# One hybrid trunk layer: mixer A's softmax on paired PSUM banks, its normalising on GpSimd, PSUM pooled anew per mixer

## Chip, cores and metric

The kernel runs as one launch on one core of a Trainium2 chip. The metric is the device time of the whole launch in microseconds; lower is better. The median of three runs of the kernel before is 1003.18 us.

## What is computed

One layer of a diffusion backbone for 128 context tokens and 512 latent tokens, model width 1024, everything in float32 at the interfaces:

```
h = RMSNorm(x) * (1 + scale1) + shift1
aq, ak, av, bq, bk, bv, ga, gb = split(h @ w_in)        # A: 8 query heads on 2 key heads; B: 8 heads
A: softmax(q k / 8) v over 512 latent + 128 cached keys  # a 128 x 640 score tile per head and query tile
B: the same over a window of the latent grid (with a learned bias) + 128 cached keys   # 384 or 512 wide
m = sigmoid(ga) * (A @ w_br_a) + sigmoid(gb) * (B @ w_br_b);  x = x + gate1 * (m @ w_out)
x = x + gate2 * (relu(h2 @ w1) ** 2 @ w2),  h2 = RMSNorm(x) * (1 + scale2) + shift2;  final RMSNorm
```

Context tokens attend to context keys only.

## The kernel before, in words

All activations lie with features on the 128 partitions and the 640 tokens along the free axis, in two halves of 320 (`HT`). A float32 product is made of three fast ones: each operand is cut into a high and a low part, and `gemm_k` (L335) adds high x high (L339), high x low (L340) and low x high (L341). One "half tile" of a weight tile is 8 of these triples into one PSUM bank. A weight tile is loaded by SyncE (L235), its high part is made by ScalarE (L301) and its low part by GpSimd or VectorE (L302); for the input projection it is GpSimd, one 128x1024 subtraction (`WPOOLSET`).

The attention stage lies at about 75 to 350 us, mixer A first (to about 220), then mixer B. For every head it goes over four query tiles. `HeadA.S` (L629) makes one 128x640 score tile as two banks of 320 columns, two matmuls each (L639, L640); VectorE takes a maximum of each bank (L641) and the smaller of the two negated ones (L642); ScalarE takes two exponentials with row sums (L644); VectorE adds the sums (L645); `normalise` (L616) takes the reciprocal (L618) and multiplies the tile on VectorE (L619). `HeadA.T` (L650) then turns the four probability tiles of a head around on TensorE (L653), `p_split` cuts them into a high part on ScalarE (L606) and a low part on VectorE (L607), and the product with the values goes into `po` (L660, L661). `HeadB` has one bank per score tile, a fused bias and maximum (L696), one exponential (L699), and the same `normalise`. `CtxPair` does the context queries of two heads.

`attention` (L921) pipelines by one head: step i of a head issues `T(i)` of the head before, `S(i)` of this one, the value product of the last `T`, and then `F.spend`, which issues some matmuls of the other input-projection tiles, the filler (`fill_tile`, L788), up to a budget (`STEP`). Mixer A's stage issues eight filler tiles, that is 16 half tiles (those of `AFILL`, and the first of `BFILL`); the last head pair has none left. A half tile is read out of its bank by ScalarE (L813, or L553 and VectorE's L554 for mixer B's queries). `F.posts` holds what follows a tile: norm and rotary of queries (L532 to L560), mixer B's key stacks (L565, L566), value stacks (L594 to L599).

PSUM has one pool for the whole kernel, by tag: `g` 2 banks (filler), `s` 3 (scores), `t` 2 (transposes), `o` 1 (value products); the norm of a query tile and the transposes of a value tile take a `g` bank too. The order of the instructions on each engine in this stage is not written by hand: the framework's planner simulates the program with its own costs and lets each engine take the earliest traced instruction that is ready. GpSimd has, beside the low parts, the low parts of mixer A's queries (L560) and DMA issues of its own queue (L577, L824, L838).

Of the kernel before, what the change touches and what calls it, by code (L numbers as in the profile page):

```python
# [10 lines left out]
F32 = mybir.dt.float32  # L11
# [5 lines left out]
P = 128  # L17
NT = 640          # tokens: 128 context, then 512 latent (column-major on the grid)
HT = 320          # tokens per half
KT = 8            # feature tiles of the model width  # L20
EPS = 1e-6
FIRST = (4, 0, 5)                                 # input tiles: mixer A keys, first queries, values
AFILL = (1, 10, 2, 6, 3, 14, 21)                      # ... next to mixer A
BFILL = (11, 7, 15, 12, 8, 16, 13, 9, 17, 29, 22, 30)         # ... next to mixer B
# [33 lines left out]
def trunk_layer(ctx: ExitStack, tc: tile.TileContext, xT, small_in, wmodA, wmodB, tabs, cacheK, cacheV, bias,  # L58
# [10 lines left out]
    pp = ctx.enter_context(tc.tile_pool(name="pp", bufs=1, space=bass.MemoryType.PSUM))  # L69
# [27 lines left out]

    def ps_g():
        return pp.tile([P, 512], F32, tag="g", bufs=2, name="pg")

    def ps_s():
        return pp.tile([P, 512], F32, tag="s", bufs=3, name="pss")

    def ps_t():
        return pp.tile([P, 512], F32, tag="t", bufs=2, name="pt")

    def ps_o():
        return pp.tile([P, 512], F32, tag="o", bufs=1, name="po")
# [55 lines left out]
    def sq_add(acc, x, f, sl):  # L164
        """sum of squares over the feature tiles but the last, whose squares are returned"""
        q = acc if f == 0 else u("sq")
        ACT.activation(q[:, sl], x[:, sl], AF.Square)
        if 0 < f < KT - 1:
            DVE.tensor_add(acc[:, sl], acc[:, sl], q[:, sl])
        return q  # L170
# [32 lines left out]
    later = []                                       # work put off until the next product  # L203
# [10 lines left out]
    class Weights:  # L214
        def __init__(self):
            self.order = list(w_order())
            self.pos = {k: i for i, (k, _) in enumerate(self.order)}
            self.loads = []                              # (key, source, number of the pair's tile)
            for key, src in self.order:
                if key[0] in BLOCKS:  # L220
                    if src is not None and key[0] == "A11":
                        self.loads += [((key[1], e), src[e], e) for e in range(2)]
                else:
                    self.loads.append((key, src, 0))
            self.st, self.t, self.raw = {}, {}, {}
            self.nd = self.nc = self.live = self.nb = 0
            self.busy = [0, 0]
# [22 lines left out]
        def block(self, name, i):  # L250
            """one operand of the seven products, [hi | lo]"""
# [37 lines left out]
        def conv(self):  # L289
            self.feed()  # L290
            key = self.order[self.nc][0]
            if key[0] in BLOCKS:
                self.t[self.nc] = self.block(*key)
            else:
                st = self.free(key)
                if key in EXTRA:
                    hi, lo = (cur["p"].tile([P, KT, P], F32R, tag="w4" + x, bufs=1, name="w4") for x in "hl")
                else:
                    hi, lo = (wp.tile([P, KT, P], F32R, tag="w" + x, bufs=3, name="w" + x) for x in "hl")
                    self.live += 2  # L300
                ACT.activation(hi, st, AF.Copy)  # L301
                (nc.gpsimd if key in WPOOLSET else DVE).tensor_sub(lo, st, r32(hi))  # L302
                self.t[self.nc] = (hi, lo)
# [10 lines left out]
        def done(self, *key):  # L314
            """the use of one tile is over; prepare the next one"""
# [39 lines left out]
    def modulate(todo, rstd, h, between=None):  # L355
        """for each (dst, x, s, sh): dst = the two parts of x * s * rstd + sh"""
# [22 lines left out]
    def warm(n):  # L379
        """keeps the tensor engine's clock up while it has to wait"""  # L380
# [3 lines left out]
    def mod_product(f, q):  # L384
        """silu(c) @ w_mod for the shift and scale of feature tile f; partial sums in four column groups"""
# [34 lines left out]
    def first_gemm(f, i, part):  # L420
        """the products of h's part with one weight tile; both parts of the tile take the high part of h"""
# [105 lines left out]
    def qk_norm(raw, g, h, bank=ps_g, src=None, buf=None):  # L527
# [23 lines left out]
    def q_part(qs, e, sl, src):  # L551
        """hi of src / 8 in the head's own partitions, lo in the other ones"""
# [4 lines left out]
    def qa_part(qs, e, raw, eng):  # L557
        """the same of mixer A's queries, whose gain holds the 1 / 8"""
# [3 lines left out]
    def k_part(k, e, dst, src, eng=None):  # L562
        """own half of the stacks k[0] = [hi; hi], k[1] = [lo; lo]"""
# [4 lines left out]
    def k_both(k, e, dst, src):  # L568
        """both halves of the stacks, the other one by the engines as well"""
# [13 lines left out]
    def v_stack(raw, cvp, bank=ps_g):  # L583
        """per key tile (ctx, lat 0..3, cache): [hi 64 | lo 64] of each of the pair's heads; in two pieces"""
# [25 lines left out]
    def combine(dst, ps, n):  # L610
        """dst (64 partitions, float32) = ps[0:64] + ps[64:128]"""
# [4 lines left out]
    def normalise(p, sm):  # L616
        rc = small("rc", 1)
        DVE.reciprocal(rc, sm)  # L618
        DVE.tensor_scalar(p, p, rc, None, op0=OP.mult)  # L619

    class HeadA:
        """512 latent queries of one head of mixer A on the latent and the cached keys"""
# [6 lines left out]
        def S(self, qt):  # L629
# [4 lines left out]
            ps = [ps_s(), ps_s()]  # L634
            p = u("pa")
            n2, s2, nm, sm = small("n2"), small("s2"), small("nm", 1), small("sm", 1)
            for j in range(2):
                c = slice(P + j * HT, P + (j + 1) * HT)
                PE.matmul(ps[j][:, :HT], q, kh[:, c], start=True, stop=False)  # L639
                PE.matmul(ps[j][:, :HT], q, kl[:, c], start=False, stop=True)  # L640
                DVE.tensor_reduce(n2[:, j:j + 1], ps[j][:, :HT], axis=AX.X, op=OP.max, negate=True)  # L641
            DVE.tensor_tensor(nm, n2[:, 0:1], n2[:, 1:2], op=OP.min)  # L642
            for j in range(2):
                ACT.activation(p[:, HALVES[j]], ps[j][:, :HT], AF.Exp, bias=nm, accum_out=s2[:, j:j + 1])  # L644
            DVE.tensor_add(sm, s2[:, 0:1], s2[:, 1:2])  # L645
# [21 lines left out]
    BQ = ((P, 384, 1, 256), (P, 512, 0, 0), (384, 512, 0, 128), (512, 384, 1, 0))   # keys, width, bias tile, columns  # L667
    BL = (0, 0, 1, 2)                                        # first local key tile of each query tile
    BG = (((4, 0, 4),), ((0, 0, 2), (3, 2, 4)), ((1, 0, 3),), ((2, 1, 4),))         # (key tile, query tiles)

    class HeadB:
        """512 latent queries of one head of mixer B on their window and the cached keys"""
# [56 lines left out]
    class CtxPair:  # L729
        """the context queries of two heads on the context keys"""  # L730
# [56 lines left out]
    # the other input tiles, interleaved with attention  # L787
    def fill_tile(n, F):  # L788
# [7 lines left out]
        for h in range(2):  # L796
# [17 lines left out]
            F.flush(1)  # L814
        F.flush()
# [32 lines left out]
    class Filler:  # L848
        """projection work that runs between the steps of attention, as far as memory allows"""
# [25 lines left out]
        def spend(self, ns):  # L875
            self.debt += ns
            while self.debt > 0:
                c = self.step()
                if c is None:
# [15 lines left out]
    # mixer A's keys, first queries and values, from the tiles computed with the first norm  # L895
# [22 lines left out]
    k_both(AK[1], 1, slice(0, NT), kraw)  # L918
    F.spend(EARLY)

    def attention(units):  # L921
        prev = pend = None
        for cur_u in units + [None]:
            if cur_u is not None:
# [54 lines left out]
    def late_mods():  # L979
        """shifts, scales and gates but the first norm's, on VectorE"""  # L980
# [30 lines left out]
    def mod_pace(used, pe=3220):  # L1011
        """as many steps as VectorE has time for next to one product"""
# [65 lines left out]
    def order(n, tail):  # L1078
        """units (tile, half): the last `tail` tiles with the first half ahead"""
# [5 lines left out]
    def unit(w, x, h):  # L1085
        """one product of a weight tile with half the tokens, with pieces of side work in its midst and behind it"""
# [50 lines left out]
    def relu2(dst, src, h):  # L1137
        """the two parts of relu(src) ** 2"""
# [15 lines left out]
    # Winograd's form of a 2 x 2 product: feature tiles 0-3 and 4-7, token halves, two weight tiles  # L1154
# [49 lines left out]
    def winograd(i, hid):  # L1204
        """hidden tiles i, i + 1 by seven products of half the depth and half the tokens"""
# [69 lines left out]
def _tiles(w, n0, n1):  # L1275
    """[K, N] -> [tiles of 128 columns, 128, K] with the contraction index k * 128 + p at [p, k, n]"""
# [18 lines left out]
def _bias_index():  # L1295
    """indices into [15 * 31 relative offsets | masked | zero]: [128 queries, 1280 key columns]"""
# [75 lines left out]
```

## Time and profile before

| | |
|---|---|
| runs | 1003.18, 1002.87, 1005.73 us; median 1003.18 us |
| span of the profiled execution, first to last instruction | 1001.3 us; the page gives the span alone, so the median lies 1.9 us over it |
| TensorE (PE) busy | 955.0 us, 95% |
| VectorE (DVE) busy | 705.0 us, 70% |
| ScalarE (ACT) busy | 517.6 us, 52% |
| GpSimd (POOL) busy | 173.5 us, 17% |
| DMA | 108.47 MB, mean 108 GB/s |

Busy time is the union of an engine's instructions. Matmuls are pipelined: each has a row of some 300 ns, and one follows the other in half of that, so TensorE can be busy by its rows without running dense; the number of matmuls per microsecond of a stretch tells the rest. An instruction's row includes the time in which it holds its engine and waits for a port.

### The profile page before, as it was taken

Reading aid. Unit: us, or ns where it says so; the run is one execution under the profiler, and the core shown is the slowest. Engines: PE = TensorE matmul, PEld = TensorE weight load, DVE = VectorE, ACT = ScalarE, POOL = GpSimd, SP = SyncE. Lnnn points to the kernel's source line nnn. Section 1 sums busy time; section 2 is a strip of 40 time slices with the busy share of each in tenths; the row PEclk is TensorE's granted clock in tenths of the full one; section 3 lists DMA queues with packets and bytes.
Section 4 is the critical chain, followed back from the end, with each engine's and each line's share of the span. In section 5 each row is a group of like instructions: output and inputs, shape, how many; then the busy total and the mean of one; then the engine's idle time right before and its main releaser. Section 6 shows DMA issues by size and latency. Waiting matters only on the chain.

```text
span 1001.3 us, 16554 instructions
## 1 busy us (share of the span) xinstructions
PE 955.0 (95%) x6317; PEld 908.8 (91%) x6317; DVE 705.0 (70%) x1576; ACT 517.6 (52%) x1117; POOL 173.5 (17%) x154
## 2 busy tenths in 40 slices
PE   7979899999899999999999999999999999999996
PEld 5778778978889999999998899999999999999896
DVE  4479898788866789788587677778733884368644
ACT  5475676668655564654324564237611662156542
POOL 0352232212231011201132100012200220012100
PEclk9999899999999999999999899999999999999999
DMA  9942101312543455556742153212320233120302
GB/s 347 208 172 69 31 25 44 77 43 77 135 111 103 133 160 189 181 169 185 224 126 81 47 164 110 85 43 84 106 78 28 85 106 88 60 79 29 126 22 105
DMA packets 34767, 108.47 MB, mean 108 GB/s; under 512 B 4320, under 2 KB 8032, under 8 KB 34688
## 3 DMA queue, kind: packets, MB, share of 16 engines
q1 hardware_dynamic: 27072, 82.63, 26.5%
q0 software_dynamic: 6464, 23.47, 8.1%
q10 hardware_dynamic: 1152, 1.31, 0.4%
q8 instruction: 49, 0.80, 0.3%
q14 instruction: 30, 0.25, 0.1%
HBM read 99.14 MB, written 4.60 MB: 104 GB/s over the span
## 4 chain that ended last, share of the span: by engine, by line
PE 65%; DVE 15%; ACT 8%; issue 3%; DMA 1%; POOL 0%; ACTq 0%; DVEq 0%; POOLq 0%; SPq 0%
PE pg L339 7%; PE pg L340 7%; PE pg L341 7%; PE pss L340 7%; PE pss L341 7%; PE pss L339 6%; PE pt L339 4%; PE pt L341 4%; PE pt L340 4%; DVE sr L260 3%; ACT wb L280 2%; PE pt L653 1%; PE pt L710 1%; DMA wst<-w 1%; DVE n L641 1%
## 5 line engine op out<-in xcount | busy, mean ns | idle before, releaser
L301 ACT ACTIVATE wh<-wst 128x1024 fp32r<-128x1024 f32 x84 | 88.8, 1057 | 112.4 <-PE pg L340 37.9
L302 DVE TENSOR_TENSOR wl<-wst,wh 128x1024 fp32r<-128x1024 f32 x53 | 64.8, 1223 | 67.5 <-ACT wh L301 67.4
L302 POOL TENSOR_TENSOR wl<-wst,wh 128x1024 fp32r<-128x1024 f32 x31 | 75.1, 2423 | 160.0 <-ACT wh L301 151.5
L992 DVE SCALAR_TENSOR_TENSOR mt<-wmt,cb 128x512 f32<-128x512 f32 x128 | 81.4, 686 | 0.0
L281 POOL TENSOR_TENSOR wb<-wst,wb 128x512 fp32r<-128x512 f32 x24 | 31.7, 1322 | 263.4 <-ACT wb L280 226.6
L339 PE MATMUL pss<-hidh,wh 128*128 128x320 f32 x216 | 67.0, 310 | 0.7 <-ACT hidh L1143 0.7
L340 PE MATMUL pss<-hidl,wh 128*128 128x320 f32 x216 | 67.0, 310 | 0.3
L341 PE MATMUL pss<-hidh,wl 128*128 128x320 f32 x216 | 66.7, 309 | 0.0
L607 DVE TENSOR_TENSOR pl<-pt,ph 128x512 fp32r<-128x512 f32 (+2 forms) x80 | 50.5, 633 | 18.3 <-ACT ph L606 17.3
L606 ACT ACTIVATE ph<-pt 128x512 fp32r<-128x512 f32 (+2 forms) x80 | 44.2, 555 | 28.8 <-PE pt L710 11.7
L280 ACT ACTIVATE wb<-sr 128x512 fp32r<-128x512 f32 x48 | 29.8, 627 | 51.5 <-DVE sr L260 35.6
L1150 DVE TENSOR_TENSOR hidl<-rl,hidh 128x320 fp32r<-128x320 f32 x64 | 37.5, 586 | 25.2 <-ACT hidh L1143 24.6
L988 POOL DMA_DIRECT2D wmt<-wmodB x32 | 17.1, 536 | 174.6 <-DVE mt L992 108.0
L340 PE MATMUL pg<-hidl,wh 128*128 128x320 f32 x144 | 44.7, 310 | 2.2 <-DVE hidl L1150 2.2
L281 DVE TENSOR_TENSOR wb<-sr,wb 128x512 fp32r<-128x512 f32 x48 | 36.0, 755 | 14.2 <-ACT wb L280 14.1
L339 PE MATMUL pg<-hidh,wh 128*128 128x320 f32 x144 | 44.7, 310 | 0.0
L341 PE MATMUL pg<-hidh,wl 128*128 128x320 f32 x144 | 44.5, 309 | 0.0
L340 PE MATMUL pt<-hidl,wh 128*128 128x320 f32 x136 | 42.1, 310 | 1.1 <-DVE hidl L1150 1.1
L341 PE MATMUL pt<-hidh,wl 128*128 128x320 f32 x136 | 42.0, 309 | 0.0
L339 PE MATMUL pt<-hidh,wh 128*128 128x320 f32 x136 | 42.0, 309 | 0.0
L644 ACT ACTIVATE pa<-pss,nm 128x320 f32<-128x320 f32 x64 | 33.1, 522 | 17.2 <-DVE nm L642 17.0
L339 PEld LDWEIGHTS pss<-hidh,wh 128*128 128x128 f32 x216 | 40.5, 188 | 1.5 <-ACT hidh L1143 1.5
(957 smaller groups left out, 3469.9 us busy)
## 6 DMA issues: line engine op xcount, KB each, us to landing
wst<-w SPq DMA_DIRECT2D x64, 512.0 KB, 3.6
wmt<-wmodB POOLq DMA_DIRECT2D x32, 512.0 KB, 4.2
wst<-w_in SPq DMA_DIRECT2D x31, 512.0 KB, 3.6
ms<-wmodA SPq DMA_DIRECT2D x16, 512.0 KB, 8.8
x<-xT SPq DMA_DIRECT2D x16, 320.0 KB, 6.1
bt<-bias SPq DMA_DIRECT2D x16, 320.0 KB, 3.3
wst<-w_br SPq DMA_DIRECT2D x8, 512.0 KB, 4.4
wst<-w_out SPq DMA_DIRECT2D x8, 512.0 KB, 3.5
```

The costliest lines, as they stand in the source:

```text
L280: ACT.activation(t[:, lo4], src, AF.Copy)
L281: later.append(lambda: (nc.gpsimd if name in BLKP else DVE).tensor_sub(t[:, hi4], src, r32(t[:, lo4])))
L301: ACT.activation(hi, st, AF.Copy)
L302: (nc.gpsimd if key in WPOOLSET else DVE).tensor_sub(lo, st, r32(hi))
L339: PE.matmul(ps, wh[:, k], xh[:, sl], start=first, stop=False)
L340: PE.matmul(ps, wh[:, k], xl[:, sl], start=False, stop=False)
L341: PE.matmul(ps, wl[:, k], xh[:, sl], start=False, stop=last)
L606: ACT.activation(ph[:, :n], pt[:, :n], AF.Copy)
L607: DVE.tensor_sub(pl[:, :n], pt[:, :n], r32(ph[:, :n]))
L644: ACT.activation(p[:, HALVES[j]], ps[j][:, :HT], AF.Exp, bias=nm, accum_out=s2[:, j:j + 1])
L992: DVE.scalar_tensor_tensor(t, st[:, q * 512:(q + 1) * 512], 1.0, r32(cb[2 * q + i][:, :512]), op0=OP.mult, op1=OP.mult, accum_out=parts[:, ...
L1150: DVE.tensor_sub(dst[1][:, sl], r[:, :HT], r32(dst[0][:, sl]))
```

## The change

In mixer A's stage the eight banks are pooled anew as two pairs for scores (`S`, 2 x 2 banks), two for transposes, one for value products and one for the filler; ahead of mixer B the pool of before is opened again. A bank of a new pool waits only for the old tiles that lay on it. A score tile of mixer A is one pair, with one maximum over both banks and one exponential. `normalise` multiplies on GpSimd, for mixer A and mixer B. The filler yields 0 behind each half tile, and in mixer A's stage `spend` returns there, with its remaining budget kept for the next step. GpSimd's low part of an input-projection tile is made in two 128x512 pieces. Norms of queries and transposes of values take a `t` bank where the pairs are in use. (Comments that the change removes are left out.)

```diff
-    pp = ctx.enter_context(tc.tile_pool(name="pp", bufs=1, space=bass.MemoryType.PSUM))
+    banks = ExitStack()
+    ctx.callback(banks.close)
+    BANKS = {"pp": {"g": 2, "s": 3, "t": 2, "o": 1}, "pa": {"S": 2, "t": 2, "o": 1, "g": 1}}
+    psum = {}
+
+    def open_banks(kind, name):
+        banks.close()
+        psum["p"] = banks.enter_context(tc.tile_pool(name=name, bufs=1, space=bass.MemoryType.PSUM, reuse_waits="tile"))
+        psum["n"] = BANKS[kind]
+
+    open_banks("pp", "pp")
...
+    def ps_2():
+        return psum["p"].tile([P, 2, 512], F32, tag="S", bufs=2, name="pss")
+
     def ps_s():
-        return pp.tile([P, 512], F32, tag="s", bufs=3, name="pss")
+        return ps_("s", "pss") if "s" in psum["n"] else ps_2()[:, 0]
...
-                (nc.gpsimd if key in WPOOLSET else DVE).tensor_sub(lo, st, r32(hi))
+                if key in WPOOLSET:
+                    for ks in (slice(0, 4), slice(4, KT)) if key[0] == "in" else (slice(0, KT),):
+                        nc.gpsimd.tensor_sub(lo[:, ks], st[:, ks], r32(hi[:, ks]))
+                else:
+                    DVE.tensor_sub(lo, st, r32(hi))
...
+    def ps_x():
+        return ps_t() if "S" in psum["n"] else ps_g()
+
-    def qk_norm(raw, g, h, bank=ps_g, src=None, buf=None):
+    def qk_norm(raw, g, h, bank=ps_x, src=None, buf=None):
-    def v_stack(raw, cvp, bank=ps_g):
+    def v_stack(raw, cvp, bank=ps_x):
...
     def normalise(p, sm):
         rc = small("rc", 1)
         DVE.reciprocal(rc, sm)
-        DVE.tensor_scalar(p, p, rc, None, op0=OP.mult)
+        nc.gpsimd.tensor_scalar(p, p, rc, None, op0=OP.mult)
...
-            ps = [ps_s(), ps_s()]
+            ps = ps_2()[:, :, :HT]
             p = u("pa")
-            n2, s2, nm, sm = small("n2"), small("s2"), small("nm", 1), small("sm", 1)
+            nm, sm = small("nm", 1), small("sm", 1)
             for j in range(2):
                 c = slice(P + j * HT, P + (j + 1) * HT)
-                PE.matmul(ps[j][:, :HT], q, kh[:, c], start=True, stop=False)
-                PE.matmul(ps[j][:, :HT], q, kl[:, c], start=False, stop=True)
-                DVE.tensor_reduce(n2[:, j:j + 1], ps[j][:, :HT], axis=AX.X, op=OP.max, negate=True)
-            DVE.tensor_tensor(nm, n2[:, 0:1], n2[:, 1:2], op=OP.min)
-            for j in range(2):
-                ACT.activation(p[:, HALVES[j]], ps[j][:, :HT], AF.Exp, bias=nm, accum_out=s2[:, j:j + 1])
-            DVE.tensor_add(sm, s2[:, 0:1], s2[:, 1:2])
+                PE.matmul(ps[:, j], q, kh[:, c], start=True, stop=False)
+                PE.matmul(ps[:, j], q, kl[:, c], start=False, stop=True)
+            DVE.tensor_reduce(nm, ps, axis=AX.XY, op=OP.max, negate=True)
+            ACT.activation(p.rearrange("p (a b) -> p a b", a=2), ps, AF.Exp, bias=nm, accum_out=sm)
             normalise(p, sm)
...
             F.flush(1)
+            yield 0
         F.flush()
...
                 c = self.step()
+                if c == 0 and "S" in psum["n"]:
+                    return
                 if c is None:
...
+    open_banks("pa", "pa")
     F.spend(EARLY)
...
         for cur_u in units + [None]:
+            if isinstance(cur_u, HeadB) and "S" in psum["n"]:
+                pend()
+                pend = None
+                open_banks("pp", "pb")
```

More of the change, by code (lines that the diff above doesn't have):

```diff
@@ L96, in small, with ps_ @@
         return sp.tile([P, n], F32, tag=f"s{n}", bufs=bufs, name=name)
+    def ps_(tag, name):
+        return psum["p"].tile([P, 512], F32, tag=tag, bufs=psum["n"][tag], name=name)
     def ps_g():
-        return pp.tile([P, 512], F32, tag="g", bufs=2, name="pg")
+        return ps_("g", "pg")
+    def ps_2():
+        return psum["p"].tile([P, 2, 512], F32, tag="S", bufs=2, name="pss")
     def ps_s():
-        return pp.tile([P, 512], F32, tag="s", bufs=3, name="pss")
+        return ps_("s", "pss") if "s" in psum["n"] else ps_2()[:, 0]
     def ps_t():
-        return pp.tile([P, 512], F32, tag="t", bufs=2, name="pt")
+        return ps_("t", "pt")
     def ps_o():
-        return pp.tile([P, 512], F32, tag="o", bufs=1, name="po")
+        return ps_("o", "po")
     def r32(ap):
```

## Prediction, made before the changed kernel was run

> **What bounds the kernel now.** I read the page first, then the busy times by stretch, then the chain, the waits and the groups of mixer A's stretch.
>
> ```profile
> span 1001.3 us, 16554 instructions
> ...
> PE 955.0 (95%) x6317; PEld 908.8 (91%) x6317; DVE 705.0 (70%) x1576; ACT 517.6 (52%) x1117; POOL 173.5 (17%) x154
> ...
> PE 65%; DVE 15%; ACT 8%; issue 3%; DMA 1%; POOL 0%; ACTq 0%; DVEq 0%; POOLq 0%; SPq 0%
> ```
>
> By busy time TensorE is full, yet a quarter of the chain that ended last is VectorE and ScalarE. The busy times by stretch say where (x is the number of instructions):
>
> ```profile
> core 0: us, PE busy (x) PEld busy (x) DVE busy (x) ACT busy (x) POOL busy (x), PEclk, DMA share, GB/s
> 75.00:220.00 145.00, 133.61 (x788) 116.39 (x788) 120.39 (x310) 93.79 (x255) 36.64 (x26) 0.95 0.19 49
> 220.00:300.00 80.00, 74.12 (x473) 66.70 (x473) 62.42 (x179) 52.50 (x133) 20.63 (x18) 1.00 0.39 101
> 300.00:350.00 50.00, 50.00 (x333) 46.77 (x332) 33.78 (x94) 28.99 (x70) 4.56 (x5) 1.00 0.38 119
> 600.00:700.00 100.00, 100.00 (x683) 100.00 (x683) 75.65 (x147) 45.50 (x88) 9.53 (x7) 1.00 0.26 84
> ```
>
> Per matmul mixer A's stretch takes 145 / 788 = 184 ns, mixer B's first part 80 / 473 = 169 and its last part, a similar mix with TensorE never idle, 50 / 333 = 150. At 150 ns mixer A's 788 would need 118 us: 27 us could be won there, and 473 x 19 ns = 9 in mixer B. The MLP's stretch (146 ns) gives nothing, and the change leaves it alone. VectorE is busy 83% of mixer A's stretch, the nearest to a bound beside TensorE. The chain by line there, and in its second half:
>
> ```profile
> by line: PE pg L339 7.7%; PE pg L340 7.2%; PE pt L653 7.2%; PE pg L341 7.1%; DVE n L641 6.7%; PE pss L639 5.2%; ACT pa L644 5.1%; DVE pl L607 4.8%; DVE pa L619 4.5%; PE po L661 4.5%; DVE nm L642 4.4%; PE po L660 4.1%; PE pss L640 3.2%; DVE
> ...
> by line: PE pg L339 7.2%; PE pg L341 7.1%; PE pg L340 6.8%; PE pt L653 6.6%; ACT pa L644 6.6%; DVE n L641 6.5%; DVE pa L619 6.3%; PE pss L639 5.4%; PE po L661 5.2%; DVE pl L607 4.7%; DVE sm L645 4.3%; DVE nm L642 4.1%; DVE bkl L566 3.5%; is
> ```
>
> So the softmax's VectorE steps are on the chain, and one of them is a minimum of two numbers per partition. The groups and one timeline show why it costs so much:
>
> ```profile
> L641 DVE TENSOR_REDUCE n<-pss 128x1 f32<-128x320 f32 x64 | 30.8, 483 | 7.1 <-PE pss L640 6.9
> L619 DVE TENSOR_SCALAR pa<-pa,rc 128x640 f32<-128x640 f32 x32 | 17.6, 551 | 0.2
> L642 DVE TENSOR_TENSOR nm<-n 128x1 f32<-128x1 f32 x32 | 10.1, 315 | 0.1
> L645 DVE TENSOR_TENSOR sm<-s 128x1 f32<-128x1 f32 x32 | 8.6, 269 | 5.3 <-ACT pa L644 5.0
> L566 DVE TENSOR_TENSOR bkl<-raw,bkh 64x512 fp32r<-64x512 f32 x4 | 3.1, 776 | 0.1
> ...
> 205.36 2.56 POOL L302 TENSOR_TENSOR wl<-wst,wh 128x1024 fp32r<-128x1024 f32 x1 [9.84 <-ACT wh L301]
> 205.62 2.33 DVE L642 TENSOR_TENSOR nm<-n 128x1 f32<-128x1 f32 x1
> ```
>
> The minimum begins 0.26 us behind GpSimd's subtraction and ends with it (207.95 against 207.92): a VectorE operation on two SBUF operands stands still while GpSimd works in SBUF.
>
> **The change part by part, mixer A.** The minimum goes: 4.4% of 145 us = 6.4 us of chain. The sum's addition goes: 4.3% of the half's 70 us = 3.0 (more, if the first half has some). Two maxima become one over 640 columns, and two exponentials one. For their slopes:
>
> ```profile
> L696 DVE CUSTOM_DVE_ANT_0 pss<-pss,bt 128x512 f32<-128x512 f32 x16 | 11.0, 687 | 0.6 <-issue 0.3 <-PE pss L693 0.3
> L696 DVE CUSTOM_DVE_ANT_0 pss<-pss,bt 128x384 f32<-128x384 f32 x15 | 8.3, 556 | 5.8 <-PE pss L693 5.7
> L699 ACT ACTIVATE pb<-pss,nm 128x512 f32<-128x512 f32 x16 | 11.0, 686 | 3.9 <-DVE nm L698 3.8
> L699 ACT ACTIVATE pb<-pss,nm 128x384 f32<-128x384 f32 x15 | 8.7, 580 | 8.0 <-DVE nm L698 7.8
> L644 ACT ACTIVATE pa<-pss,nm 128x320 f32<-128x320 f32 x64 | 33.1, 522 | 17.2 <-DVE nm L642 17.0
> ```
>
> VectorE from PSUM takes 131 / 128 = 1.02 ns a column, so one maximum takes an estimated 483 + 327 = 810 ns against 966: 16% of 6.7% of 145 us is 1.6 us of chain. ScalarE: 106 / 128 = 0.83 ns a column, 522 + 265 = 787 against 1044, a quarter of 7.4 us; with the sums' readout, which stays once, I take 1.5.
>
> Normalising moves from VectorE (551 ns) to GpSimd. No row shows GpSimd with one tensor operand. Its rows:
>
> ```profile
> L302 POOL TENSOR_TENSOR wl<-wst,wh 128x1024 fp32r<-128x1024 f32 x15 | 36.4, 2424 | 96.8 <-ACT wh L301 88.4 <-PE pt L653 6.8 <-PE po L660 1.5
> L281 POOL TENSOR_TENSOR wb<-wst,wb 128x512 fp32r<-128x512 f32 x24 | 31.7, 1322 | 263.4 <-ACT wb L280 226.6 <-DVE x L1100 36.8
> L560 POOL TENSOR_TENSOR qs<-raw,qs 64x640 fp32r<-64x640 f32 x7 | 11.2, 1597 | 28.3 <-ACT qs L559 28.0
> L577 POOL DMA_DIRECT2D bkh<-bkh x8 | 4.2, 527 | 8.4 <-DVE nm L642 8.3
> ```
>
> With two operands and 640 columns it takes 1597 ns, an upper bound; VectorE's 551 is the lower. I take 1.0 us, near the middle, since one operand is read and not two. The chain's 4.5% (6.5 us) then becomes 11.8: 5.3 us lost. The Trainium skill ("GPSIMD Engine Reference", Elementwise — side-by-side cycle accounting) gives 1.8 cycles an element at 1.2 GHz as GpSimd's best loop; an estimate from it is 0.96 us and a loss of 4.8.
>
> The sum by line is -6.4 - 3.0 - 1.6 - 1.5 + 5.3 = -7.2 us. Three effects lie beside it.
>
> *The queue on VectorE.* It loses 30.8 + 17.6 + 10.1 + 8.6 = 67.1 us and gets 32 x 0.81 = 26: 41 of 120 us. In return GpSimd is busy 36.6 + 32 = 69 us instead of 37, and the two-operand work that stays (key stacks such as L566, rotary) is held up more often: with the minimum's excess, 315 - 150 ns at 25% busy, twice that for some 40 instructions is 13 us. Net 28 us. Chain lines such as L607 (4.8%, 7 us) are partly queueing; I credit 4 us. The skill ("SBUF — State Buffer", Who interferes with whom) calls the shared port an exclusive lock that whoever issues first keeps for the whole instruction. The timeline above agrees (2.33 us); by that rule each of the new GpSimd instructions is such a lock too, which is what speaks most against this part.
>
> *Banks.* The waits in mixer A's stretch:
>
> ```profile
> PEld pss L639 <- ACT pa L644: 8.2, 13, 2.0
> PEld pt L653 <- DVE pa L619: 5.0, 9, 1.0
> PEld pg L339 <- ACT raw L813: 1.5, 3, 0.7
> ...
> L813 ACT ACTIVATE raw<-pg 128x320 f32<-128x320 f32 x11 | 4.6, 433 | 1.5 <-PE pg L341 1.5
> ```
>
> TensorE's loads wait 8.2 us for a score bank: three banks hold one and a half tiles, two pairs hold two. I credit 3 us. The filler pays with its second bank: after each of 16 half tiles TensorE must find other work while ScalarE reads out (0.43 us and its turn). The half-tile stop puts a step of scores, transposes and value products there, so I charge 0.2 us each, 3 us; uncovered it is 1.3 us (readout, one other ScalarE operation of about 0.6, the handover) or 21. And mixer B's filler can no longer be drawn ahead into the last heads of mixer A, since its banks open later: 1 us.
>
> Mixer A: -7.2 - 4 - 3 + 3 + 1 = -10 us.
>
> **Mixer B.** Only the normalising and GpSimd's halves change.
>
> ```profile
> L619 DVE TENSOR_SCALAR pb<-pb,rc 128x384 f32<-128x384 f32 x16 | 8.9, 557 | 0.2
> L619 DVE TENSOR_SCALAR pb<-pb,rc 128x512 f32<-128x512 f32 x16 | 7.7, 483 | 0.1
> ...
> PEld pt L710 <- DVE pb L619: 0.9, 2, 0.7
> ```
>
> VectorE loses 16.6 of 96 us. The fourth tile of a head is needed at once by the next head's first transposes, and comes some 0.4 us later: 8 x 0.4 = 3 us at most, against about 3 us of freer VectorE. Queued behind a normalise that waits are GpSimd's low parts and the DMA issues (0.53 us each: key copies, context outputs), and the reverse; weights are cut two tiles ahead, so the filler hides that. Zero. Two pieces of 1.32 us instead of one of 2.42 cost GpSimd 0.2 us a tile and shorten each hold. Opening the banks twice drains little, since banks wait one by one: zero, at most 2 us.
>
> Total -10 us on the span of 1001.3: 991.3; with the 1.9 us that lie around it, 993.2. I forecast **993**.
>
> **Rivals.** *Dense (0.12).* If the softmax is all that thins TensorE out, mixer A reaches mixer B's last 150 ns a matmul: -27 us, 976. For: VectorE falls from 83% to some 64%. Against: the last heads have no filler.
>
> *No change (0.09).* TensorE waits for the fourth tile's normalising in both mixers as long as it now waits for maxima; gains and losses cancel, 1002. For: loads already wait 5.0 us in 9 cases for L619.
>
> *Late normalising, slower (0.16).* GpSimd is in order. If a normalise takes 1.6 us (mixer B's about 1.25) and stands behind a weight piece half the time (0.65), the fourth tile is 1.05 + 0.65 = 1.7 us late at 8 head ends in mixer A and 0.75 + 0.65 = 1.4 at 8 in mixer B: 25 us, against 15 of gains left (the sum without its 5.3): +10, 1013. It decides from about 1 us per head end. Against: the planner has filler to put there, if its price for GpSimd is right.
>
> *One filler bank, slower (0.09).* The stop doesn't cover the readout: 21 us instead of 3, so -10 + 18 = +8, 1011. It decides from 0.8 us per half tile.
>
> **How the numbers follow.** The forecast has 0.54 and its own range is 985 to 999. A measurement tells 0.3%, 3 us, from no change. Faster: 0.54 + 0.12 = 0.66; the same 0.09; slower 0.25. A range from 978 to 1010 leaves out about half of the dense case (0.06) and most of the two slower ones' upper parts (0.14).
>
> **What would show it.** Right: in mixer A's stretch L642 and L645 are gone, VectorE is near 90 us busy, the stretch from the first to the last mixer A exponential is some 10 us shorter, 640-wide maxima take 0.8 us, and GpSimd's normalise about 1.0; the MLP's stretch keeps 146 ns a matmul. Wrong: transposes L653 or L710 wait for GpSimd more than 10 us in all (late normalising); filler matmuls wait for L813 more than 10 us (one bank); a normalise above 1.4 us; or mixer B longer by what mixer A gains.

## The result: 3.15% slower

The changed kernel takes 1035.44 us in the median (1032.88 to 1035.77) against 1003.88 for the kernel before in the same comparison: a ratio of 1.0315, 95% interval 1.0287 to 1.0342. The forecast was 993 us and the range ended at 1010. The page of the changed kernel (line numbers are its own now: `normalise` multiplies in L643, the scores are L663 and L664, the maximum L665, the exponential L666, `HeadA.T` L674, `HeadB.T` L731):

```profile
span 1033.5 us, 16532 instructions
...
PE 961.0 (93%) x6317; PEld 914.9 (89%) x6317; DVE 662.4 (64%) x1416; ACT 512.1 (50%) x1053; POOL 282.7 (27%) x237
...
PE 47%; DVE 9%; ACT 7%; issue 3%; DMA 1%; POOL 0%; ACTq 0%; DVEq 0%; SPq 0%; POOLq 0%
```

VectorE lost 43 us of work, as meant, and GpSimd got 109 more. Beware of the chain here: its shares add up to 67%, so it breaks off, and GpSimd is missing from it. The busy times by stretch hold the loss:

```profile
75.00:220.00 145.00, 124.43 (x741) 111.38 (x742) 84.10 (x162) 83.61 (x184) 94.62 (x63) 0.94 0.15 43
220.00:300.00 80.00, 69.70 (x428) 62.25 (x427) 47.13 (x140) 46.50 (x118) 41.59 (x35) 0.95 0.27 80
300.00:350.00 50.00, 47.50 (x310) 43.90 (x309) 25.83 (x71) 26.82 (x63) 24.57 (x22) 1.00 0.33 96
600.00:700.00 100.00, 100.00 (x681) 99.66 (x681) 73.27 (x155) 42.19 (x78) 4.42 (x5) 1.00 0.27 90
```

With VectorE at 58% of mixer A's stretch TensorE does 741 matmuls there instead of 788; mixer B's parts fall from 473 and 333 to 428 and 310; the MLP's stretch is as before. The exponentials of mixer A (`pa`) and mixer B (`pb`) mark the stages: count, shortest/median/longest in ns, first and last start. Before, then the changed kernel:

```profile
L644 ACT ACTIVATE pa<-pss,nm x64: 508/522/537, 79.5 to 216.6; 128x320 f32<-128x320 f32 x64
L699 ACT ACTIVATE pb<-pss,nm x32: 566/628/691, 219.2 to 339.5; 128x384 f32<-128x384 f32 x16, 128x512 f32<-128x512 f32 x16
...
L666 ACT ACTIVATE pa<-pss,nm x32: 779/795/822, 80.3 to 222.5; 128x640 f32<-128x640 f32 x32
L720 ACT ACTIVATE pb<-pss,nm x32: 573/640/691, 239.0 to 367.7; 128x384 f32<-128x384 f32 x16, 128x512 f32<-128x512 f32 x16
```

Mixer A takes 142.2 us instead of 137.1, mixer B 128.7 instead of 120.3, and between them lie 16.5 us instead of 2.6. Behind the last exponential 665.8 us follow instead of 661.8. So the loss of 32 us in the span is about 5 + 14 + 8 + 4, and two things stand out in the trace: a wait for GpSimd, and the hole between the mixers. The groups of GpSimd, and TensorE's waits from 75 to 380 us:

```profile
L643 POOL TENSOR_SCALAR pa<-pa,rc 128x640 f32<-128x640 f32 x32 | 61.2, 1919 | 23.0 <-DVE rc L642 21.3 <-PE pss L664 1.5
L643 POOL TENSOR_SCALAR pb<-pb,rc 128x512 f32<-128x512 f32 x16 | 25.1, 1567 | 14.8 <-DVE rc L642 14.8
L643 POOL TENSOR_SCALAR pb<-pb,rc 128x384 f32<-128x384 f32 x16 | 19.9, 1244 | 27.4 <-DVE rc L642 26.6 <-PE pg L361 0.5 <-PE pss L714 0.2
...
PE pt L674 <- POOL pa L643: 15.9, 13, 3.0
PE pt L731 <- POOL pb L643: 10.3, 12, 1.7
```

A normalise takes 1.92 us on GpSimd, not 1.0, and TensorE waits 26 us for it in all. The shortest of mixer A's takes 1.87 us, so this is the instruction's own length and not a wait in a few of them.

### The profile page after: what moved, and what is told of

Read it like the earlier page. It is cut to its first block, busy times and chain, and to the rows that moved or that the text cites. A ratio compares the mean times of both kernels' runs of the same rounds, so it can differ in the third digit from the quotient of the medians.

```text
span 1033.5 us, 16532 instructions
## 1 busy us (share of the span) xinstructions
PE 961.0 (93%) x6317; PEld 914.9 (89%) x6317; DVE 662.4 (64%) x1416; ACT 512.1 (50%) x1053; POOL 282.7 (27%) x237
## 4 chain that ended last, share of the span: by engine, by line
PE 47%; DVE 9%; ACT 7%; issue 3%; DMA 1%; POOL 0%; ACTq 0%; DVEq 0%; SPq 0%; POOLq 0%
PE pss L361 6%; PE pss L362 6%; PE pss L360 6%; PE pg L360 5%; PE pg L361 5%; PE pg L362 5%; PE pt L361 4%; PE pt L360 4%; PE pt L362 4%; DVE sr L277 4%; ACT wb L297 3%; DVE wb L298 1%; DMA wst<-w 1%; ACT rl L1171 1%; ACT rl L1169 1%
## 5 line engine op out<-in xcount | busy, mean ns | idle before, releaser
L321 POOL TENSOR_TENSOR wl<-wst,wh 128x512 fp32r<-128x512 f32 (+1 forms) x50 | 77.3, 1562 | 98.8 <-ACT wh L318 98.0
L643 POOL TENSOR_SCALAR pa<-pa,rc 128x640 f32<-128x640 f32 x32 | 61.2, 1919 | 23.0 <-DVE rc L642 21.3
L643 POOL TENSOR_SCALAR pb<-pb,rc 128x384 f32<-128x384 f32 (+1 forms) x32 | 45.0, 1405 | 42.3 <-DVE rc L642 41.4
L674 PE MATMUL pt<-pk,pa 128*128 128x128 f32 x160 | 29.6, 298 | 17.5 <-POOL pa L643 15.9
L674 PEld LDWEIGHTS pt<-pk,pa 128*128 128x128 f32 x160 | 21.3, 151 | 24.5 <-POOL pa L643 19.9
```

Source lines behind the costliest of these rows:

```text
L321: nc.gpsimd.tensor_sub(lo[:, ks], st[:, ks], r32(hi[:, ks]))
L643: nc.gpsimd.tensor_scalar(p, p, rc, None, op0=OP.mult)
L674: PE.transpose(pt[:, qt * P:(qt + 1) * P], self.p[qt][:, t * P:(t + 1) * P], ident)
```

## Experiments

**Theory N**: the slow normalise holds up the transposes. **Theory B**: the banks, opened anew and with one for the filler, keep TensorE from drawing filler ahead. Each run's ratio is to the kernel before, in runs on the same chip (its medians there were 1003.65 to 1005.21 us), with its 95% interval. The intervals reach some 0.25% to either side, and many of the runs were made on different chips, so a difference between two experiments is known to 3 or 4 us; where medians and ratios give two values, both are named.

### Normalise back on VectorE

```diff
-        nc.gpsimd.tensor_scalar(p, p, rc, None, op0=OP.mult)
+        DVE.tensor_scalar(p, p, rc, None, op0=OP.mult)
```

> The changed kernel with one edit undone: the normalising multiplication goes back to VectorE. Theory N (the slow GpSimd normalise, 1919 ns for 640 columns in the changed kernel's trace against 551 on VectorE, holds the fourth tile's transposes): the 26 us in which TensorE waited for it go, and the pairs' gain appears, 995 to 1008 us. Theory B (the banks: one filler bank and pools opened anew leave TensorE without filler ahead of mixer A and in its last heads): most of the loss stays, 1018 to 1030 us.

1013.76 us, 1.0091 (1.0063 to 1.0118). It lies between the two theories' ranges: 22 us of the loss go with the normalise, and some 9 stay.

### The kernel before, normalising on GpSimd

The opposite edit in the kernel before, nothing else.

> The kernel before with one edit: normalising multiplies on GpSimd. Banks, maxima, exponentials and filler as before. Theory N: slower by 20 us or more, 1023 to 1035 us. Theory B: the filler, with its two banks and free to be drawn ahead, covers the later tiles; at most 8 us slower, 1003 to 1011 us.

1030.37 us, 1.0261 (1.0222 to 1.0300): +26 us, as theory N has it, against 22 in the changed kernel. The filler, though free to be drawn ahead, does not cover it. TensorE's waits there:

```profile
PE pt L653 <- POOL pa L619: 20.3, 18, 2.3
PE pt L710 <- POOL pb L619: 8.9, 13, 1.3
```

### Only the fourth tile of a head on VectorE

```diff
-            normalise(p, sm)
+            normalise(p, sm, DVE if qt == 3 else None)      # else GpSimd; the same in mixer B
```

> The changed kernel, but the fourth query tile of each head is normalised on VectorE; the other three stay on GpSimd. Theory N in the form of the prediction (only the fourth tile is urgent): as good as all four on VectorE, 995 to 1008 us. If GpSimd's throughput counts (three tiles of 1.9 us in a head's time, and its low parts behind them), it lies between the changed kernel and the all-VectorE one. Theory B: 1018 to 1030 us.

1016.88 us, 1.0123 (1.0102 to 1.0144). It is above theory N's range, which ended at 1008. Of the 22 us, nearly 19 come back by moving a quarter of the tiles, and TensorE's waits for GpSimd's normalise fall from 26.2 to 9.7 us. That fits the fourth tile's lateness, as the rival of the prediction had it, with a few us for GpSimd's throughput; moving another quarter of the tiles, which would tell the two apart, was not tried.

### A cheaper form on GpSimd

```diff
-        nc.gpsimd.tensor_scalar(p, p, rc, None, op0=OP.mult)
+        nc.gpsimd.tensor_tensor(p, p, rc.broadcast_to([P, p.shape[1]]), op=OP.mult)
```

> The changed kernel, whose normalising on GpSimd is a multiplication of two tensors, the reciprocal broadcast along the row, in place of tensor times scalar. By the two-operand row of the kernel before (1597 ns for 640 columns on 64 partitions, against 1919 for the scalar form) each takes 1.6 us in mixer A and 1.05 to 1.35 in mixer B, and the time falls by 6 to 15 us, 1020 to 1029 us. If a broadcast operand is read no faster than a scalar is applied: 1.9 us and 1032 to 1038 us.

1019.87 us, 1.0141 (1.0114 to 1.0168), 15.6 us less than the changed kernel (17 by the ratios) and just under the range that I had expected. Its normalises in mixer A and mixer B:

```profile
L643 POOL TENSOR_TENSOR pa<-pa,rc x32: 1245/1255/1690, 81.4 to 214.7; 128x640 f32<-128x640 f32 x32
L643 POOL TENSOR_TENSOR pb<-pb,rc x32: 817/931/1043, 229.3 to 354.7; 128x384 f32<-128x384 f32 x16, 128x512 f32<-128x512 f32 x16
```

The same multiplication takes 1255 ns as tensor times broadcast tensor and 1886 as tensor times scalar: two thirds, and less than the 1.6 us that I had expected. On VectorE the kernel is still 5 or 6 us faster.

### The pools opened anew, alone

In the kernel before the pool is closed and opened again with its own layout, so that nothing differs but the seam: at both places, only ahead of mixer A, only ahead of mixer B.

```diff
+    open_banks("pa")                       # ahead of mixer A: both, and e5
     F.spend(EARLY)
...
+            if isinstance(cur_u, HeadB) and not opened:      # ahead of mixer B: both, and e6
+                pend()
+                pend = None
+                open_banks("pb")
```

> The kernel before, whose PSUM pool of 2 + 3 + 2 + 1 banks is closed and opened again with the same layout at the two places where the change does it (ahead of mixer A's stage, and ahead of mixer B with the pending value product issued first). Nothing else. Theory B: the filler can't be drawn ahead over the two seams, 6 to 15 us slower, 1010 to 1018 us. Theory N: the seams cost nothing, 1002 to 1006 us.

> The kernel before with its PSUM pool closed and opened again, same layout, only ahead of mixer A's stage. If a seam costs what it keeps the filler from being drawn ahead: in the kernel with both seams TensorE waited 10.0 us for the first scores, after 38 matmuls between 56 and 75 us where the kernel before had 72 filler matmuls. So 6 to 9 us slower, 1010 to 1013 us. If the seams cost by the drain at mixer B alone: 1003 to 1006 us.

> The same with the seam only ahead of mixer B (pending value product first). In the kernel with both seams 12.1 us lay between the last exponential of mixer A and the first of mixer B, against 2.0 in the kernel before. If that is this seam's whole price, 9 to 12 us slower, 1013 to 1016 us, and the two seams add up to the 18 us of both. If the seams share a price, less.

Both: 1023.04 us, 1.0188 (1.0160 to 1.0217), more than either theory gave it. Ahead of mixer A: 1005.13 us, 1.0005 (0.9989 to 1.0020), nothing, against my 6 to 9 us, though TensorE waits 10.1 us there for the first scores' query tile from GpSimd, where the kernel before waits 4.2: that wait, which is 9.5 us in the changed kernel, is not part of the loss. Ahead of mixer B: 1021.28 us, 1.0151 (1.0130 to 1.0173), nearly all of it, and more than the 9 to 12 us that I had read from the hole. The exponentials with the seam ahead of mixer B:

```profile
L653 ACT ACTIVATE pa<-pss,nm x64: 506/523/534, 83.1 to 218.1; 128x320 f32<-128x320 f32 x64
L708 ACT ACTIVATE pb<-pss,nm x32: 567/634/691, 232.0 to 358.9; 128x384 f32<-128x384 f32 x16, 128x512 f32<-128x512 f32 x16
```

The hole of 13.9 us is there without pairs and without the normalise on GpSimd, and mixer B takes 126.9 us instead of 120.3. Two things changed at it. First, ScalarE's read-out of mixer B's query tiles, four readings to a tile, between 75 and 240 us, in the kernel before, with the seam, and in the changed kernel:

```profile
L553 ACT ACTIVATE qs<-pg x8: 416/432/432, 121.2 to 209.6; 64x320 fp32r<-64x320 f32 x8
...
L562 ACT ACTIVATE qs<-pg x6: 417/432/435, 125.3 to 237.3; 64x320 fp32r<-64x320 f32 x6
...
L577 ACT ACTIVATE qs<-pg x4: 421/432/434, 126.4 to 141.0; 64x320 fp32r<-64x320 f32 x4
```

Before, the planner had drawn mixer B's second tile ahead, into mixer A's last heads, which have no filler of their own; over the seam it does not. Second, mixer B's first scores against mixer A's last value products, before and with the seam:

```profile
L692 PE MATMUL pss<-bkh,qs x32: 337/421/505, 216.8 to 336.9; 128*128 128x384 f32 x16, 128*128 128x512 f32 x16
L661 PE MATMUL po<-pl,vst x40: 389/393/657, 94.1 to 228.2; 128*128 128x512 f32 x40
...
L701 PE MATMUL pss<-bkh,qs x32: 337/408/486, 229.6 to 356.3; 128*128 128x384 f32 x16, 128*128 128x512 f32 x16
L670 PE MATMUL po<-pl,vst x40: 387/394/793, 97.7 to 229.1; 128*128 128x512 f32 x40
```

Before, the scores begin 11.4 us ahead of the last value product; with the seam 0.5 us behind it. The edit itself has a hand in this, since it issues the pending value product ahead of mixer B.

### Without the stop at half tiles

```diff
-                if c == 0 and "S" in psum["n"]:
-                    return
```

> The changed kernel with normalising on VectorE and without the filler's stop at half tiles; seams and pairs stay. If the stop covers the readout of the single filler bank, as the prediction had it, it is slower without: 1015 to 1025 us against 1013.8 with it. If the planner moves filler about anyway, within 3 us of 1013.8.

In the kernel with VectorE's normalise: 1013.57 us, 1.0086 (1.0058 to 1.0113), against 1013.76 with the stop. The stop does nothing that these runs can tell.

### No seam: pairs through both mixers

```diff
-    open_banks("pp", "pp")
+    open_banks("pa", "pa")
...
-            ps = ps_s()
+            if qt % 2 == 0:
+                self.pair = ps_2()
+            ps = self.pair[:, qt % 2]               # in HeadB
```

> The changed kernel with normalising on VectorE and no seam: the paired layout (two pairs, two transposes, one value, one filler bank) is there from the first norm on through both mixers, and is exchanged only ahead of the merge; mixer B takes the two halves of a pair for two query tiles. If seams and the GpSimd normalise are the whole loss, the pairs' own gain of about 9 us is left (18 of seams less 9 measured with them): 992 to 999 us. If the single filler bank costs as much as the pairs bring, 1001 to 1008 us.

1025.51 us, 1.0197 (1.0174 to 1.0221): a miss. Its exponentials:

```profile
L668 ACT ACTIVATE pa<-pss,nm x32: 776/796/808, 83.6 to 211.0; 128x640 f32<-128x640 f32 x32
L724 ACT ACTIVATE pb<-pss,nm x32: 573/634/692, 216.9 to 355.5; 128x384 f32<-128x384 f32 x16, 128x512 f32<-128x512 f32 x16
```

Mixer A is at 127.4 us, 9.7 less than before, and the hole is 5.9; but mixer B takes 138.6 instead of 120.3. Without a seam, and with one filler bank and scores that free a bank only in pairs, mixer B loses more than the seam costs. Which of the two it is was not tried. Here, too, the planner draws mixer B's second query tile ahead only in part: the first of its four readings begins at 206.7 us and the last at 230.3, where the kernel before has the last at 209.6. So the seam is not the only thing that can keep that filler back.

### The filler tile issued early

```diff
-            self.allowed = len(AFILL)
+            self.allowed = len(AFILL) + 1
...
-                    F.allowed += 3
+                    F.allowed += 3 if cur_u.j else 2
```

In the VectorE-normalising version, in the kernel before with the seam, and in the changed kernel as it is:

> The changed kernel with normalising on VectorE, and mixer B's second query tile (16 filler units of three matmuls) issued in mixer A's last heads: one more tile is allowed there, one fewer when mixer B begins. Seams, pairs and stop stay. Theory F (the seam ahead of mixer B costs the filler that the planner drew ahead over it; in the kernel before it read out that tile by 209.6 us, before mixer B's first exponential): 7 to 14 us faster than the 1013.8 without it, 1000 to 1007 us, and the gap between the mixers' exponentials, 13.4 us, falls under 6. Theory D (the seam itself drains the engines): 1012 to 1016 us.

> The kernel before with the pool opened again ahead of mixer B, and that same filler tile issued in mixer A's last heads. Theory F: the seam's 15 to 16 us mostly vanish, 1004 to 1010 us. Theory D: 1019 to 1023 us.

> The changed kernel as it is, normalising on GpSimd, with the filler tile issued in mixer A's last heads. Theory F: 8 to 14 us faster than 1035.4, 1021 to 1027 us. If the last heads wait for GpSimd so that TensorE's order stalls in any case, less, 1028 to 1034 us. Theory D: 1033 to 1037 us.

1011.42 us, 1.0059 (1.0037 to 1.0082): 2.3 us, which these runs do not tell from nothing, and the hole stays (mixer A's last exponential ends at 216.2, mixer B's first begins at 229.9). 1012.77 us, 1.0081 (1.0055 to 1.0108): 8.5 us (7 by the ratios), half of the seam. 1029.60 us, 1.0238 (1.0209 to 1.0267): 5.8 us (8 by the ratios). The first two lie between the ranges of the two theories: the filler is part of the seam's price, not all of it.

The granted clock of TensorE differs at this place as well. From 200 to 240 us, in the kernel before, with the seam, and with the seam and the early tile (the clock stands behind POOL's busy time):

```profile
200.00:240.00 40.00, 37.50 (x222) 31.66 (x220) 34.55 (x101) 27.00 (x75) 6.56 (x5) 0.96 0.25 66
200.00:240.00 40.00, 32.09 (x151) 25.21 (x149) 27.73 (x83) 20.52 (x61) 1.04 (x2) 0.79 0.17 44
200.00:240.00 40.00, 31.85 (x173) 25.44 (x173) 28.74 (x84) 23.07 (x62) 5.33 (x5) 0.91 0.18 49
```

With fewer matmuls in the stretch (222, 151 and 173) the clock is lower too (0.96, 0.79 and 0.91). What the lower clock alone costs was not told apart.

### Pools split, so that only score and filler banks are exchanged

```diff
+    px = ctx.enter_context(tc.tile_pool(name="px", bufs=1, space=bass.MemoryType.PSUM))
...
-        return psum["p"].tile([P, 512], F32, tag=tag, bufs=psum["n"][tag], name=name)
+        return (px if tag in "to" else psum["p"]).tile([P, 512], F32, tag=tag, bufs=psum["n"][tag], name=name)
...
-                pend()
-                pend = None
                 open_banks("pp", "pb")
```

In the kernel before with the seam ahead of mixer B, in the changed kernel with VectorE's normalise, in the latter with the early filler tile, and in that with mixer A's first three tiles normalised by GpSimd's two-tensor form:

> The kernel before with transposes and value products in a PSUM pool of their own that stays open; only the score and filler banks are opened again ahead of mixer B, and the pending value product is not issued early. Theory D2 (the seam makes mixer B's first scores wait until mixer A's last transposes and value products are out of their banks, which lie in the pool that closes): those no longer count, and of the 15 to 17 us of that seam at most 4 are left, 1003 to 1008 us, with under 5 us between the mixers' exponentials. If any reopening drains the order at that place: 1015 to 1022 us.

> The changed kernel with normalising on VectorE, and the same split of the pools: only score and filler banks are exchanged between pairs and singles. Theory D2: the seam's price goes from the 1013.8 of that kernel and the pairs' gain shows, 996 to 1003 us. Otherwise 1010 to 1015 us.

> The same with the filler tile of mixer B issued in mixer A's last heads. If the filler still can't be drawn over the seam, this gives some 2 to 8 us more than the split alone: 990 to 1000 us. If the open seam lets the planner draw it ahead, as much as the split alone, 996 to 1003 us.

> The same, but the first three query tiles of a mixer A head are normalised on GpSimd by a two-tensor multiplication (1255 ns where it was used for all), the fourth and all of mixer B on VectorE. VectorE is relieved of 24 x 0.55 = 13 us in mixer A's stretch. If only the fourth tile is urgent: 0 to 5 us faster than all on VectorE. If GpSimd's hold on the port costs VectorE as much as it is relieved of: 0 to 6 us slower.

1015.81 us, 1.0106 (1.0086 to 1.0125): 5.5 us of the seam's (4.5 by the ratios), less than theory D2 expected and within the range for a drain by any reopening; mixer B's first scores now begin 7 us ahead of mixer A's last value product, and the filler is still not drawn. 1006.88 us, 1.0013 (1.0001 to 1.0025), and 1004.60 us, 0.9993 (0.9979 to 1.0008): both as fast as the kernel before, the first between its two ranges, the second above both of its own. 1003.59 us, 0.9985 (0.9970 to 1.0000), which these runs do not tell from the version before it.

### One filler bank kept open, too

```diff
-    BANKS = {"pp": {"g": 2, "s": 3, "t": 2, "o": 1}, "pa": {"S": 2, "t": 2, "o": 1, "g": 1}}
+    BANKS = {"pp": {"g": 1, "h": 1, "s": 3, "t": 2, "o": 1}, "pa": {"S": 2, "t": 2, "o": 1, "g": 1}}
...
-        return (px if tag in "to" else psum["p"]).tile(...)
+        return (px if tag in "tog" else psum["p"]).tile(...)        # the filler takes g and h in turn
```

With the early filler tile and without it:

> The mixed normalising kernel with pairs (1003.6 us) and one filler bank that stays open with transposes and value products; ahead of mixer B only the two pairs are exchanged for three score banks and a second filler bank. If what is left of the seam (6.9 us between the mixers' exponentials, against 2.0 in the kernel before) is filler that can't start: 2 to 5 us faster, 998 to 1002 us. If it is the score banks' exchange: 1002 to 1006 us.

> The same without the extra filler tile in mixer A's last heads. If a filler bank that stays open lets the planner draw that tile ahead by itself, as fast as with it, 998 to 1003 us; if not, 2 to 5 us slower than with it.

With it 998.24 us (997.84 to 999.95), a ratio of 0.9953 (0.9940 to 0.9966): faster than both kernels. Without it 1004.60 us, 1.0007 (0.9995 to 1.0019): with an open bank alone the planner draws only part of the tile ahead (the first of its four readings begins at 200.7 us, the other three from 222.1 on). The early tile and the open bank were not tried without the pairs. The faster one's exponentials:

```profile
L671 ACT ACTIVATE pa<-pss,nm x32: 773/795/808, 81.6 to 209.6; 128x640 f32<-128x640 f32 x32
L725 ACT ACTIVATE pb<-pss,nm x32: 561/638/690, 217.5 to 332.7; 128x384 f32<-128x384 f32 x16, 128x512 f32<-128x512 f32 x16
```

Mixer A 128.0 us, mixer B 115.2; a hole of 7.9 us is still there. From 200 to 240 us TensorE does 249 matmuls, and the granted clock is 1.00.

## Why the prediction was wrong

The loss has three parts: the normalise on GpSimd +22 us (the changed kernel against e1), the seams +19 (e4), the pairs with all that comes with them -10 (e1 against e4: 1.0091 against 1.0188). These three lie on one chain from the kernel before to the changed one, so that they must add up to the measured 31.6, and their sum proves nothing. Other pairs of runs check each part: the normalise alone costs 26 us in the kernel before (e2); the seam ahead of mixer B alone 15 to 17 (e6); the pairs bring 9 again with the pools split (e16 against e14), but only 1 to 2 with the early tile (e9 against e10). So the parts depend on each other by several us.

*Normalising, "I take 1.0 us".* This step failed first. 1.92 us lies outside the bounds that I had called upper and lower: here an operation with two operands was no upper bound for one with a scalar. GpSimd's scalar form grows by (1919 - 1244) / 256 = 2.6 ns a column, the two-operand subtraction by (2424 - 1322) / 512 = 2.15. The Trainium skill's best loop ("GPSIMD Engine Reference", Elementwise — side-by-side cycle accounting), 0.96 us by my estimate, is half of what the trace shows. The mechanism was written down as the rival "late normalising", with the right place, L674 and L731: TensorE's 26 us of waits are 1.6 us at each of 16 head ends, over its threshold of 1 us. Its price of 25 us was close to the 22 to 26 measured, in part by luck: it took 1.6 us for a normalise that takes 1.9, and the weight piece that it put in front of half of them was not measured. Its chance, 0.16, hung on the bound.

*Mixer B, "Zero".* It failed with the same term: TensorE waits 10.3 us there for L643. Mixer B's 8 us more are not the normalise's alone, however: with the normalise alone (e2) mixer B takes 126.5 us, with the seam alone (e6) 126.9, against 120.3.

*"Opening the banks twice drains little ... at most 2 us", and "1 us" for filler not drawn ahead.* This step failed by nearly as much. The seam ahead of mixer B costs 15 to 17 us (e6). The split pools take back 4.5 to 5.5 of it (e14 against e6), the filler tile issued early 7 to 8.5 (e10 against e6); the rest, and what the lower granted clock adds (0.79 against 0.96), was not told apart. That a bank of a new pool waits only for what lay on it is a rule on waits; the order that the planner wrote put mixer B's first scores behind mixer A's last value product in every kernel that closed the whole pool there. These kernels also issue the pending value product first, and the split drops that as well, so which of the two holds the scores back, and whether for a bank or for the pool, was not tried.

*"One filler bank", 3 us, and the stop that covers it.* The waits for the read-out in the changed kernel are small, and the stop has no effect (e8).

```profile
PEld pg L360 <- ACT raw L834: 2.8, 10, 0.4
```

*The sum by line and the queue on VectorE.* The single costs were right, the gain too large and partly in another place. The maximum takes 812 ns (I had 810), the exponential 795 (787), VectorE falls to 84 us of mixer A's stretch (I had near 90). Without the normalise's 5.3 us the terms came to -15 us in mixer A. There, e1 is only 3.6 us shorter than e4 (132.6 against 136.2 from first to last exponential) and e16 only 4.5 shorter than e14 (130.9 against 135.4); another 4.6 and 3.5 us lie in mixer B, which has no pairs in these kernels. What brings them, such as GpSimd's low parts in two pieces, was not tried by itself.

The Trainium skill's rule of an exclusive lock that is kept for the whole instruction ("SBUF — State Buffer", Who interferes with whom), which I weighed against the change, agrees here with GpSimd's subtractions; the new normalise keeps VectorE waiting in its first part alone. Two low parts of mixer B's key stacks in the changed kernel, one beside the low part of a query tile, one inside a normalise; last, the kernel before with the normalise on GpSimd (e2):

```profile
76.35 2.03 POOL L584 TENSOR_TENSOR qs<-raw,qs 64x640 fp32r<-64x640 f32 x1
76.98 1.55 DVE L590 TENSOR_TENSOR bkl<-ck,bkh 64x128 fp32r<-64x128 f32 x1
...
99.71 1.89 POOL L643 TENSOR_SCALAR pa<-pa,rc 128x640 f32<-128x640 f32 x1
101.07 0.28 DVE L590 TENSOR_TENSOR bkl<-raw,bkh 64x128 fp32r<-64x128 f32 x1
...
106.14 1.88 POOL L619 TENSOR_SCALAR pa<-pa,rc 128x640 f32<-128x640 f32 x1 [1.24 <-DVE rc L618]
106.48 0.46 DVE L642 TENSOR_TENSOR nm<-n 128x1 f32<-128x1 f32 x1
```

The first key stack is held until the subtraction ends; the second takes its usual 0.28 us in the midst of a normalise. In e2 the minimum, 0.15 us in the median before, is held, but only until 0.80 us after the normalise began, and not to its end. Four more minima there show the same 0.80 us, and of what began more than 0.6 us into a normalise only one instruction was held. In the changed kernel one of VectorE's instructions on two SBUF operands is held by a normalise, L567 at 174.63 us, by 0.5 us; I had charged 13 us for work held up.

*VectorE as the bound.* The reading that VectorE thins TensorE out in mixer A is borne out in part. Mixer A is 9 us shorter than before with pairs through both mixers (127.4 against 137.1 us) and in the fastest kernel (128.0), but with the early filler tile e9 is no shorter than e10 (136.1 and 136.3). How much filler a kernel does inside mixer A moves this time as well.

## What to carry to other kernels

Do not bound an operation on another engine by a different form of it: measure the form, or leave the range open upwards, and ask first whether its result is the last thing that the next stage waits for. A pool that is closed and opened in the midst of a pipeline can be a seam in the order even if its waits are fine-grained; try keeping open what the tail of one stage and the head of the next both use, and look at what a planner had drawn over that place. When a change bundles a gain with two losses, undo its parts one by one, and in more than one order: here the pairs brought 1 to 10 us by what stood beside them. With the losses removed the kernel was as fast as before, and with a filler tile issued early, a filler bank kept open and GpSimd normalising three tiles of four it is 0.5% faster.

## Hardware behaviour that I had not expected

GpSimd multiplies 128x640 float32 by a per-partition scalar in 1886 ns in the median, and by the same scalar broadcast as a second tensor in 1255. VectorE's L619 does it in 551 in the mean. The slower form is the better neighbour: in e2 it held VectorE's work on two SBUF operands only in its first 0.8 us, while in e12 a key stack of 0.28 us that began 0.22 us into a two-tensor normalise of 0.83 took 0.74, until that was over.
